# A two-layer encoder trunk on one core: the second mixer's scores as four products over all 128 rows, its rotation ended a unit later, its outputs turned in three parts, and the first mixer's mask added on VectorE

## The chip, the core and the metric

The kernel runs on one core of a Trainium2 chip. The metric is device time in microseconds (us) of one execution of the whole program. The kernel before takes 1678.19 us, the median of 3 runs (1677.85 to 1679.21). All times below are of that kernel.

The engines: TensorE (PE in the profile; PEld is its weight load) multiplies and turns blocks, VectorE (DVE) and ScalarE (ACT) work element by element on PSUM and SBUF, GpSimd (POOL) and SyncE (SP) mostly issue DMAs here. Each engine runs its own instructions in a fixed order and waits for the others by semaphores.

## What is computed

Two sequences (256 and 512 rows, held as six tiles of 128 rows: tiles 0 and 1, tiles 2 to 5) go through two layers. Each layer is a token mixer and a SwiGLU, both between norms:

```python
for i in range(DEPTH):                       # DEPTH = 2
    h = rms_norm(x, norm_mix_pre[i])
    if i % 2 == 0:
        m = window_gqa_sink(h, a_w_in, a_w_o, a_sinks)     # first mixer
    else:
        m = diff_attention(h, b_w_in, b_w_o, ...)          # second mixer
    x = x + rms_norm(m, norm_mix_post[i])
    h = rms_norm(x, norm_ffn_pre[i])
    x = x + rms_norm(swiglu(h, ffn_w_gate_up[i], ffn_w_down[i]), norm_ffn_post[i])
```

```python
# first mixer: 16 query heads, 4 key heads of 64; only |q - k| <= 128 counts
sc = where(valid, q @ k.T, -inf)
m = maximum(max(sc), sink)
p = exp(sc - m) / (sum(exp(sc - m)) + exp(sink - m))
o = p @ v
# second mixer: 8 heads, each with two query and key components c of 64 and values of 128
p_c = softmax(q_c @ k_c.T)                   # all keys of the sequence
o = (p_0 - lam * p_1) @ v
o = rms_norm(o, subln) * (1 - lambda_init)   # per head
```

Everything is float32. A large product is made of three fp32r products of a high and a low part each: hi*hi, lo*hi, hi*lo.

## The kernel before

**Order.** The program is recorded as Python functions called one after the other; a scheduler then places each engine's instructions by the recorded order and by when it thinks their operands are ready. So the lists of steps in `mixer_a` and `mixer_b` set the order, and the scheduler moves rows a little. Products of 128 x 384 or 128 x 512 are the filling ("fill"), and the steps of attention are put in between them.

**First mixer** (`mixer_a`, lines 598 to 766). 24 units, one for each group of heads `gi` and tile `t`, project queries, keys and values into a PSUM bank `pqa`. Four units later a unit's attention runs as four items, one for each head. An item is `score`: two products (L661, L662) of queries with the keys' high and low parts into a bank `sc` of 256 or 384 columns (384 for tiles 3 and 4, which have a block on both sides), and one or two mask products (L664, L666): identity times a bf16 triangle of -3e38, added into the same bank. Then VectorE takes the row maximum (L668) and turns it into `negm` (L671), ScalarE takes the exponential out of PSUM with a running sum (L677) and the sink's exponential (L679). `normalize` (L686 to L688) follows one item later, `turn_e` (L697, transposes `tpe`) two items after that, and `values` (L711, `poa`) once for each unit.

**Second mixer** (`mixer_b`, lines 796 to 990). `b_fill` lists 50 units: `rotated` units project a head's queries or keys for half of the rows (bank `pqb` or `pkb`), `straight` units project values for a group of heads (`pvb`). When a rotated unit ends, ScalarE copies it out as `xq` or `xk` (L834), four DMAs from GpSimd's queue swap its quarters (L836), and VectorE forms z = s cos + r sin (L838, L839, L840), where L839 needs the four DMAs. ScalarE then rounds z to the high part (L849). For queries VectorE puts the low part into the other 64 rows (L852). For keys two DMAs copy the high part into the other 64 rows (L855) and VectorE writes the low part (L856) to its own 64 rows alone.

`score` (L879) of a head and tile makes two banks `bsc`, one for each component: a product over all 128 rows with the keys' high part (L890), which covers q_hi and q_lo at once, and one over 64 rows with the keys' low part (L893); the second component's 64 rows are the other half of the array. Then come the maximum (L896), exponential (L898), the combination of both components (L901 to L906), `turn_e` (L918, L920) and `values` (L931). After heads 3, 6 and 7 the heads so far are scaled on GpSimd (`rstd_sub` L391, `ob` L944). The list `events` says in which unit, counted in units and fractions, each score, turn and value step stands.

The outputs `o` are then turned into `h_hi` and `h_lo` as operands of the output projection (`transposes`, L438, L445, L446; bank `tp_o`), heads 0 to 3 first (`early`) and heads 4 to 7 later (`late`). What remains of the attention stands between the first products of that projection (`out`, bank `po`) in a list written out by hand (`run`).

Of the kernel before, what the change touches and what calls it, by code (L numbers as in the profile page):

```python
# [9 lines left out]
F32 = mybir.dt.float32  # L10
F32R = mybir.dt.float32r
# [6 lines left out]
P = 128  # L18
# [49 lines left out]
def trunk(  # L68
# [40 lines left out]
    ident_b = const.tile([P, P], BF16, name="ident_b")  # L109
    nc.vector.tensor_copy(out=ident_b, in_=ident)  # L110

    masks = []
    for name, step, mult in (("mask_l", 1, -1), ("mask_r", -1, 1)):
        m = const.tile([P, P], BF16, name=name)
        nc.gpsimd.memset(m, 0.0)
        nc.gpsimd.affine_select(
            out=m, in_=m, compare_op=ALU.is_ge, fill=MASK, base=0,
            pattern=[[step, P]], channel_multiplier=mult,
        )
        masks.append(m)  # L120
    cos_sb = const.tile([P, 4, HD], F32, name="cos_sb")
    sin_sb = const.tile([P, 4, HD], F32, name="sin_sb")
# [10 lines left out]
    def small_inputs():  # L133
# [4 lines left out]
        lam_in = const.tile([P, 4, HD], F32, name="lam_in")  # L138
# [5 lines left out]
    def small_tables():  # L144
# [3 lines left out]
        lprod = const.tile([P, 2, HD], F32, name="lprod")  # L148
# [449 lines left out]
    def mixer_a(gp, g_next, first_steps, o):  # L598
        with ExitStack() as st:
# [53 lines left out]
            def score(i, j):  # L653
# [6 lines left out]
                left, right = k0 < t, k1 > t + 1  # L660
                nc.tensor.matmul(s, q[i][:, j], kh[gi, first][:, keys], start=True, stop=False)  # L661
                nc.tensor.matmul(s, q[i][:, j], kl[gi, first][:, keys], start=False, stop=not (left or right))  # L662
                if left:
                    nc.tensor.matmul(s[:, :P], ident_b, masks[0], start=False, stop=not right)  # L664
                if right:
                    nc.tensor.matmul(s[:, (nk - 1) * P:], ident_b, masks[1], start=False, stop=True)  # L666
                mx = small.tile([P, 1], F32, tag="mx", name=f"mx{i}_{j}")
                nc.vector.tensor_reduce(out=mx, in_=s, axis=AX.X, op=ALU.max)  # L668
                h = gi * 4 + j
                negm = small.tile([P, 1], F32, tag="negm", name=f"negm{i}_{j}")  # L670
                nc.vector.tensor_scalar(  # L671
                    out=negm, in0=mx, scalar1=-HD ** -0.5, scalar2=nsink[:, h:h + 1], op0=ALU.mult, op1=ALU.min)
                if j % 2 == 0:
                    e2[0] = new_y(f"e{i}_{j}")
                e = e2[0][:, j % 2 * 512:j % 2 * 512 + nk * P]
                den = small.tile([P, 2], F32, tag="den", name=f"den{i}_{j}")
                nc.scalar.activation(  # L677
# [864 lines left out]
```

## Time and profile before

| what | us |
|---|---|
| median of 3 runs | 1678.19 |
| the profiled execution, its own time | 1678.24 |
| its span, first to last instruction | 1676.5 |
| first mixer's attention, about | 34 to 254 of the span |
| second mixer: units with attention | 833 to 1078 |
| second mixer: rest of the attention with the first output products | 1078 to 1135 |
| both SwiGLU parts, about | 299 to 780 and 1182 to 1676 |

Times within the profile are us from the span's start. In a timeline row stand the start, the time that the row covers, the engine, the line, the operation, output and inputs, the shape, how many instructions were merged, and in brackets the idle time of the engine before the row and what ended it. Matmuls overlap: what one costs the stream is the distance from its start to the next start, not its duration. In a row of groups stand the busy time of the group, the mean duration of one in ns, and the idle time before its members. In a row of waits stand who waited for whom, the sum, how often, and the longest.

### The profile page before, as it was taken

The page shows a single profiled execution, that of the slowest core. Times are in us where ns is not written, and L with a number is a line of the kernel's source. Part 1 is how long each engine was busy: PE and PEld are TensorE (multiplying, and loading weights), DVE is VectorE, ACT ScalarE, POOL GpSimd, SP SyncE. Part 2 cuts the span into 40 slices and gives each one's busy share as a digit, 9 for nine tenths or more (in the row PEclk, how much of TensorE's full clock was granted, in tenths as well). Part 3 has the DMA queues.
Part 4 walks back from the last instruction along what each step waited for, and adds up shares of the span by engine and source line. Part 5 has one row for each costly group of instructions (what it writes and reads, how often), then busy time and mean ns, then how long its engine had stood idle before and what let it go on. Part 6 is the DMA issues. An engine that isn't in the chain of part 4 may idle for free. (4 is left out here: it accounts for less than half of the span.)

```text
span 1676.5 us, 25190 instructions
## 1 busy us (share of the span) xinstructions
PE 1638.5 (98%) x9291; PEld 1495.1 (89%) x9291; DVE 1235.2 (74%) x2210; ACT 943.9 (56%) x2080; POOL 162.5 (10%) x276
## 2 busy tenths in 40 slices
PE   7999999999999999999999999999899999999998
PEld 7888878899999998888999989877899999998886
DVE  7888776896766656988685775765897666666985
ACT  6777775654444444556566666675744444444653
POOL 1000001000000000001330451331000000000000
PEclk9999999999999999999999999999999999999999
DMA  5111014534233337675432322314434343337664
GB/s 214 39 39 47 15 39 148 179 131 143 101 127 108 129 125 246 225 268 192 127 84 61 76 71 75 104 31 139 166 119 147 104 142 109 129 115 242 237 244 156
DMA packets 68187, 217.53 MB, mean 130 GB/s; under 512 B 9248, under 2 KB 13472, under 8 KB 67808
## 3 DMA queue, kind: packets, MB, share of 16 engines
q1 hardware_dynamic: 54576, 175.93, 30.9%
q0 software_dynamic: 13344, 39.73, 8.1%
q8 instruction: 73, 1.20, 0.3%
q14 instruction: 50, 0.41, 0.1%
q10 hardware_dynamic: 144, 0.26, 0.0%
HBM read 163.59 MB, written 42.86 MB: 123 GB/s over the span
## 5 line engine op out<-in xcount | busy, mean ns | idle before, releaser
L254 DVE TENSOR_TENSOR wlo<-wraw,whi 128x1024 fp32r<-128x1024 f32 (+2 forms) x174 | 204.6, 1179 | 176.7 <-ACT whi L253 175.2
L253 ACT CAST whi<-wraw 128x1024 fp32r<-128x1024 f32 (+2 forms) x174 | 175.8, 1012 | 119.9 <-PE py L347 59.1
L346 PE MATMUL py<-hhi,whi 128*128 128x384 f32 x464 | 155.4, 335 | 0.9 <-ACT u L1029 0.9
L348 PE MATMUL py<-hhi,wlo 128*128 128x384 f32 x464 | 155.0, 334 | 0.0
L347 PE MATMUL py<-hlo,whi 128*128 128x384 f32 x464 | 155.0, 334 | 0.0
L334 ACT CAST hhi<-araw 128x768 fp32r<-128x768 f32 (+1 forms) x74 | 57.6, 783 | 88.7 <-DMA araw<-act 85.9
L348 PE MATMUL pv<-whi,hlo 128*128 128x512 f32 (+1 forms) x240 | 92.2, 384 | 0.4 <-DVE hlo L335 0.4
L346 PE MATMUL pv<-whi,hhi 128*128 128x512 f32 (+1 forms) x240 | 92.4, 385 | 0.0
L347 PE MATMUL pv<-wlo,hhi 128*128 128x512 f32 (+1 forms) x240 | 92.2, 384 | 0.0
L335 DVE TENSOR_TENSOR hlo<-araw,hhi 128x768 fp32r<-128x768 f32 (+1 forms) x74 | 65.3, 890 | 32.3 <-ACT hhi L334 32.2
L346 PEld LDWEIGHTS py<-hhi,whi 128*128 128x128 f32 x464 | 87.1, 188 | 1.8 <-ACT u L1029 1.5
L347 PEld LDWEIGHTS py<-hlo,whi 128*128 128x128 f32 x464 | 87.1, 188 | 0.0
L348 PEld LDWEIGHTS py<-hhi,wlo 128*128 128x128 f32 x464 | 87.1, 188 | 0.0
L346 PE MATMUL po<-whi,hhi 128*128 128x512 f32 x192 | 78.8, 410 | 3.3 <-ACT hhi L445 2.9
L1082 POOL DMA_DIRECT2D act<-st x22 | 19.4, 882 | 635.9 <-DVE st L1081 635.9
L347 PE MATMUL po<-wlo,hhi 128*128 128x512 f32 x192 | 75.4, 393 | 0.8 <-DVE wlo L254 0.8
L348 PE MATMUL po<-whi,hlo 128*128 128x512 f32 x192 | 76.0, 396 | 0.2 <-DVE hlo L335 0.2
L346 PE MATMUL pqa<-whi,hhi 128*128 128x384 f32 x192 | 73.7, 384 | 0.0
L346 PE MATMUL px<-hhi,whi 128*128 128x384 f32 x208 | 70.2, 339 | 2.7 <-ACT hhi L334 2.7
L898 ACT ACTIVATE be<-bsc,bmx 128x512 f32<-128x512 f32 (+1 forms) x96 | 58.5, 614 | 24.6 <-DVE bmx L896 24.3
L347 PE MATMUL px<-hlo,whi 128*128 128x384 f32 x208 | 70.0, 337 | 1.2 <-DVE hlo L335 1.2
L391 POOL TENSOR_TENSOR rstd_post<-rstd_post,mhalf 128x1 f32<-128x1 f32 x23 | 16.4, 716 | 557.9 <-ACT rstd_post L390 557.9
(315 smaller groups left out, 5112.9 us busy)
## 6 DMA issues: line engine op xcount, KB each, us to landing
act<-st POOLq DMA_DIRECT2D x22, 1344.0 KB, 6.6
wraw<-in_wgu SPq DMA_DIRECT2D x56, 512.0 KB, 4.6
araw<-act SPq DMA_DIRECT2D x70, 384.0 KB, 4.1
y_wraw<-in_wgu SPq DMA_DIRECT2D x40, 512.0 KB, 3.8
wraw<-in_wd SPq DMA_DIRECT2D x40, 512.0 KB, 4.0
xd<-x SPq DMA_DIRECT2D x18, 512.0 KB, 3.0
x<-xd SPq DMA_DIRECT2D x18, 512.0 KB, 3.9
wraw<-in_wo SPq DMA_DIRECT2D x16, 512.0 KB, 3.5
```

What stands on the lines that cost most here:

```text
L253: state["raw_hi"] = nc.scalar.copy(out=hi, in_=src)
L254: state["raw_lo"] = nc.vector.tensor_tensor(out=lo, in0=src, in1=hi.bitcast(F32), op=ALU.subtract)
L334: state["hi"] = nc.scalar.copy(out=hi, in_=src)
L335: state["lo"] = nc.vector.tensor_tensor(out=lo, in0=src, in1=hi.bitcast(F32), op=ALU.subtract)
L346: nc.tensor.matmul(out, ah, bh, start=start and i == 0, stop=False, skip_group_check=more)
L347: nc.tensor.matmul(out, ah, bl, start=False, stop=False, skip_group_check=more)
L348: nc.tensor.matmul(out, al, bh, start=False, stop=stop and i == last, skip_group_check=more)
L391: nc.gpsimd.tensor_tensor(out=r[:, :w], in0=r[:, :w], in1=mhalf[:, :w], op=ALU.pow)
L898: nc.scalar.activation(out=e[:, :n * P], in_=s, func=AF.Exp, bias=mx, accum_out=den[:, c:c + 1])
L1082: nc.gpsimd.dma_start(out=at_hand[c // 4][:, :, c // 2 % 2], in_=out.pop(c // 2))
```

## The change

1. **Mask.** The mask products go. A float32 tile `mask` of 128 x 384 holds the two triangles with zeros between, and one VectorE instruction with a running minimum, `tensor_tensor_reduce`, reads the scores and the mask, writes (sc + mask) * -1/8 to SBUF and gives `negm`. ScalarE's exponential reads that tile instead of PSUM. The sink's exponential, its sum and the reciprocal are made once for two heads, in `normalize`, which now stands at every second item for the pair before; `turn_e` stays three items behind its score. Small tables move into a pool that is freed behind the first mixer.
2. **Scores of the second mixer.** The key tile has four parts, high and low for each component. The low part is copied to the other 64 rows too (DMAs of 64 x 2 x 384 in place of 64 x 384, issued behind the subtraction), and each bank gets two products over all 128 rows. Value tiles: 8 buffers in place of 9.
3. **Rotation.** `end` of a rotated unit stops behind the first product with the cosine. The rest runs at the end of the next unit, set behind the last combination on VectorE.
4. **Turns.** `o` is turned in three parts: heads 0 to 3, 4 to 6, and 7. The first parts of tiles 0 to 2 stand in the units 48 and 49; score events stand 0.2 to 0.8 units later, and `run` is a new list.

```diff
-                left, right = k0 < t, k1 > t + 1
-                nc.tensor.matmul(s, q[i][:, j], kl[gi, first][:, keys], start=False, stop=not (left or right))
-                if left:
-                    nc.tensor.matmul(s[:, :P], ident_b, masks[0], start=False, stop=not right)
-                if right:
-                    nc.tensor.matmul(s[:, (nk - 1) * P:], ident_b, masks[1], start=False, stop=True)
-                nc.vector.tensor_reduce(out=mx, in_=s, axis=AX.X, op=ALU.max)
-                nc.vector.tensor_scalar(
-                    out=negm, in0=mx, scalar1=-HD ** -0.5, scalar2=nsink[:, h:h + 1], op0=ALU.mult, op1=ALU.min)
-                nc.scalar.activation(
-                    out=e, in_=s, func=AF.Exp, bias=negm, scale=HD ** -0.5, accum_out=den[:, 0:1])
-                nc.scalar.activation(out=den[:, 1:2], in_=negm, func=AF.Exp, bias=sink[:, h:h + 1])
+                nc.tensor.matmul(s, q[i][:, j], kl[gi, first][:, keys], start=False, stop=True)
+                nc.vector.tensor_tensor_reduce(
+                    out=e, in0=s, in1=mask[:, side:side + nk * P], scale=-HD ** -0.5, scalar=nsink[:, h:h + 1],
+                    op0=ALU.add, op1=ALU.min, accum_out=negm[:, c])
+                nc.scalar.activation(out=e, in_=e, func=AF.Exp, bias=negm[:, c], scale=-1.0, accum_out=den[:, c])
...
             def normalize(i, j):
+                nc.vector.tensor_tensor(out=den[:, 2:4], in0=negm, in1=sink[:, h:h + 2], op=ALU.add)
+                nc.scalar.activation(out=den[:, 2:4], in_=den[:, 2:4], func=AF.Exp)
+                nc.vector.tensor_tensor(out=den[:, 0:2], in0=den[:, 0:2], in1=den[:, 2:4], op=ALU.add)
+                nc.vector.reciprocal(out=den[:, 0:2], in_=den[:, 0:2])
+                for c in range(2):
+                    e = blocks[i, j + c][0]
+                    nc.vector.tensor_scalar(out=e, in0=e, scalar1=den[:, c:c + 1], scalar2=None, op0=ALU.mult)
...
-                if 1 <= n <= n_items:
-                    normalize(*items[n - 1])
+                if n % 2 == 0 and 2 <= n <= n_items:
+                    normalize(*items[n - 2])
...
-                            nc.gpsimd.dma_start(out=b[other], in_=b[rows])
-                            nc.vector.tensor_tensor(
-                                out=kk[h][rows, 2, cols], in0=z[rows], in1=b[rows].bitcast(F32), op=ALU.subtract)
+                                c = 2 * (rows is down)
+                                nc.vector.tensor_tensor(
+                                    out=kk[h][rows, c + 1, cols], in0=z[rows], in1=b[rows].bitcast(F32), op=ALU.subtract)
+                                nc.gpsimd.dma_start(out=kk[h][other, c:c + 2, cols], in_=kk[h][rows, c:c + 2, cols])
...
+                    state["mark"] = state["z"]
+                    waiting.append(rest)
...
-                    vv[g, t] = ap.tile([P, n], F32, tag="v", name=f"vb{g}_{t}", bufs=9)
+                    vv[g, t] = ap.tile([P, n], F32, tag="v", name=f"vb{g}_{t}", bufs=8)
...
-                    nc.tensor.matmul(ss[c], qt[:, c, at], kk[h][:, c, keys], start=True, stop=False)
-
-                for c, rows in enumerate((slice(0, HD), slice(HD, P))):
-                    nc.tensor.matmul(ss[c], qt[rows, c, at], kk[h][rows, 2, keys], start=False, stop=True)
+                    for part in range(2):
+                        nc.tensor.matmul(
+                            ss[c], qt[:, c, at], kk[h][:, 2 * c + part, keys], start=part == 0, stop=part == 1)
...
-            turn_o = [transposes(o[t], t, f"o1_{t}", subl) for t in range(NT)]
+            turn_o = [[turn_heads(t, *hs) for hs in ((0, 4), (4, 7), (7, 8))] for t in range(NT)]
...
+            def turn_heads(t, k0, k1):
...
+                    for j in range(n):
+                        nc.tensor.transpose(tp[:, j * P:(j + 1) * P], o[t][:, (k0 + j) * P:(k0 + j + 1) * P], ident)
+                    nc.scalar.activation(out=h4, in_=v, func=AF.Copy, scale=subl)
+                    nc.vector.scalar_tensor_tensor(
+                        out=l4, in0=v, scalar=subl, in1=h4.bitcast(F32), op0=ALU.mult, op1=ALU.subtract)
...
+            events += [(48.3 + t / 2, "o", t) for t in range(3)]
...
+                late = waiting[:]
+                waiting.clear()
                 for s in placed(att, [int((at - i) * len(fill)) for at, _, _ in now], fill):
                     s()
+                turned(late)
```

What this moves on the engines, at three places:

VectorE in the first mixer, unit 10 (tile 4, 384 columns): `mx10_1` is the maximum of head 1, `sp` belongs to the projection, `den10_0` and `y_e10_0` to the sum and exponentials of head 0 (and 1). Before:

```order
L668 TENSOR_REDUCE mx10_1_1922<-sc10_1_1917 128x1
L627 TENSOR_TENSOR sp13_1884<-qk13_1877,sp13_1884 128x4x64
L629 TENSOR_TENSOR sp13_1884<-qk13_1877,sp13_1884 128x128
L671 TENSOR_SCALAR negm10_1_1924<-mx10_1_1922,nsink_108 128x1
L686 TENSOR_TENSOR den10_0_1900<-den10_0_1900 128x1
L687 RECIPROCAL den10_0_1900<-den10_0_1900 128x1
L688 TENSOR_SCALAR y_e10_0_1899<-y_e10_0_1899,den10_0_1900 128x384
L668 TENSOR_REDUCE mx10_2_1948<-sc10_2_1943 128x1
```

And now, where each `ISA` pair is the new instruction and its reading out:

```order
L667 ISA y_e10_0_1677,negm10_0_1678<-sc10_1_1699,mask_91,nsink_107 128x384
L667 ISA negm10_0_1678 128x1
L678 TENSOR_TENSOR den10_0_1679<-negm10_0_1678,sink_106 128x2
L624 TENSOR_TENSOR sp13_1668<-qk13_1661,sp13_1668 128x4x64
L626 TENSOR_TENSOR sp13_1668<-qk13_1661,sp13_1668 128x128
L667 ISA y_e10_2_1718,negm10_2_1719<-sc10_2_1715,mask_91,nsink_107 128x384
L667 ISA negm10_2_1719 128x1
L680 TENSOR_TENSOR den10_0_1679<-den10_0_1679 128x2
L681 RECIPROCAL den10_0_1679<-den10_0_1679 128x2
L684 TENSOR_SCALAR y_e10_0_1677<-y_e10_0_1677,den10_0_1679 128x384 x2
```

The scaling of head 0 stood ahead of the third head's maximum; now it stands behind the third head's masked minimum, together with head 1's.

GpSimd in the second mixer, where head 5's keys are rotated (`xk5_0`, `xk5_1`) while heads 0 to 3 of the tiles 3 and 4 are scaled (`rstd_sub21`, `ob3`, and so on). Before:

```order
L836 DMA xk5_0_10729<-xk5_0_10729 32x384 x2
L836 DMA xk5_1_10815<-xk5_1_10815 32x384
L855 DMA kb5_10739<-kb5_10739 64x384 x2
L391 TENSOR_TENSOR rstd_sub22_10802<-rstd_sub22_10802,mhalf_102 128x4
L836 DMA xk5_1_10815<-xk5_1_10815 32x384
L944 TENSOR_TENSOR ob4_8521<-ob4_8521,rstd_sub22_10802 128x512
L836 DMA xk5_1_10815<-xk5_1_10815 32x384 x2
```

And now:

```order
L834 DMA xk5_0_10172<-xk5_0_10172 32x384 x4
L388 TENSOR_TENSOR rstd_sub21_10225<-rstd_sub21_10225,mhalf_101 128x4
L963 TENSOR_TENSOR ob3_8008<-ob3_8008,rstd_sub21_10225 128x512
L834 DMA xk5_1_10256<-xk5_1_10256 32x384 x4
L388 TENSOR_TENSOR rstd_sub22_10308<-rstd_sub22_10308,mhalf_101 128x4
L963 TENSOR_TENSOR ob4_8009<-ob4_8009,rstd_sub22_10308 128x512
L858 DMA kb5_10266<-kb5_10266 64x2x384 x2
```

The four DMAs of `xk5_1` had a key copy, a power and a scaling between them; now they follow each other, and the key copies stand two tiles later.

TensorE at the end of the second mixer, around the first product of the output projection (`po1_0_0`). Before:

```order
L893 MATMUL bsc40_1_11839<-kb6_11432,qb6_1_11360 128x512
L438 MATMUL tp_o1_0_0_11855<-ident_81,ob0_8517 128x128 x4
L918 MATMUL tpa38_11862<-ident_81,be38_11696 128x128 x4
L931 MATMUL pob37_11869<-vb2_0_10892,aT37_11780 128x128
L931 MATMUL pob37_11869<-vb2_1_10949,aT37_11780 128x128
L438 MATMUL tp_o1_1_0_11879<-ident_81,ob1_8518 128x128 x4
L346 MATMUL po1_0_0_11833<-whi158_11209,hhi0_111 128x512
```

And now, the rows ahead of that product:

```order
L895 MATMUL bsc39_0_11305<-kb6_10993,qb6_1_10913 128x512 x2
L895 MATMUL bsc39_1_11306<-kb6_10993,qb6_1_10913 128x512 x2
L937 MATMUL tpa37_11322<-ident_81,be37_11185 128x128 x2
L950 MATMUL pob36_11327<-vb2_0_10372,aT36_11262 128x128
L950 MATMUL pob36_11327<-vb2_1_10437,aT36_11262 128x128
L343 MATMUL po1_0_0_11300<-whi158_10697,hhi0_110 128x512
```

The transposes `tp_o1_0_0`, whose result that product reads, stood five rows ahead of it and now stand 71 rows ahead, among the products of unit 48.

More of the change, by code (lines that the diff above doesn't have):

```diff
@@ L108, in trunk @@
     nc.vector.tensor_copy(out=ident_r, in_=ident)
[L109 to L115, printed above, removed]
+    early_stack = ctx.enter_context(ExitStack())
+    early = early_stack.enter_context(tc.tile_pool(name="early", bufs=1, side="right", reuse_waits="tile"))
+    mask = early.tile([P, 3 * P], F32, name="mask")
+    nc.gpsimd.memset(mask, 0.0)
+    for at, step, mult in ((0, 1, -1), (2 * P, -1, 1)):
         nc.gpsimd.affine_select(
-            out=m, in_=m, compare_op=ALU.is_ge, fill=MASK, base=0,
+            out=mask[:, at:at + P], in_=mask[:, at:at + P], compare_op=ALU.is_ge, fill=MASK, base=0,
             pattern=[[step, P]], channel_multiplier=mult,
         )
-        masks.append(m)
-    cos_sb = const.tile([P, 4, HD], F32, name="cos_sb")
-    sin_sb = const.tile([P, 4, HD], F32, name="sin_sb")
+    cos_sb = early.tile([P, 4, HD], F32, name="cos_sb")
+    sin_sb = early.tile([P, 4, HD], F32, name="sin_sb")
     mhalf = const.tile([P, 8], F32, name="mhalf")
@@ L673, in score @@
                 if j % 2 == 0:
[L674 to L677, printed above, removed]
-                    out=e, in_=s, func=AF.Exp, bias=negm, scale=HD ** -0.5, accum_out=den[:, 0:1])
-                nc.scalar.activation(out=den[:, 1:2], in_=negm, func=AF.Exp, bias=sink[:, h:h + 1])
-                blocks[i, j] = e, den
@@ L682, in mixer_a @@
-            e2 = {}
-            def normalize(i, j):
-                e, den = blocks[i, j]
-                nc.vector.tensor_tensor(out=den[:, 0:1], in0=den[:, 0:1], in1=den[:, 1:2], op=ALU.add)
-                nc.vector.reciprocal(out=den[:, 0:1], in_=den[:, 0:1])
-                nc.vector.tensor_scalar(out=e, in0=e, scalar1=den[:, 0:1], scalar2=None, op0=ALU.mult)
+                    pair[0] = (
+                        new_y(f"e{i}_{j}"), small.tile([P, 2], F32, tag="negm", name=f"negm{i}_{j}"),
+                        small.tile([P, 4], F32, tag="den", name=f"den{i}_{j}"))
@@ new lines, in score @@
+                blocks[i, j] = e, den, negm
+            pair = {}
+            def normalize(i, j):
+                h = (i // NT) * 4 + j
+                _, den, negm = blocks[i, j]
+                nc.vector.tensor_tensor(out=den[:, 2:4], in0=negm, in1=sink[:, h:h + 2], op=ALU.add)
[5 more added lines that the diff above has]
+                    nc.vector.tensor_scalar(out=e, in0=e, scalar1=den[:, c:c + 1], scalar2=None, op0=ALU.mult)
@@ L806, in mixer_b @@
             live = [0]
+            waiting = []
             def held(key, n):
@@ L848, in end @@
[L848 to L857 removed]
+                    state["z"] = nc.vector.tensor_tensor(out=z, in0=s, in1=tab[0][:, half], op=ALU.mult)
```

87 lines of the change are left out of this document (52 added, 35 removed).

## The prediction

> **What bounds the kernel now.** I read the page's table of engines first, then the table by windows for the three stretches that the change touches, then TensorE's waits there.
>
> ```profile
> PE 1638.5 (98%) x9291; PEld 1495.1 (89%) x9291; DVE 1235.2 (74%) x2210; ACT 943.9 (56%) x2080; POOL 162.5 (10%) x276
> ...
> 34.00:254.00 220.00, 219.46 (x1503) 183.54 (x1502) 172.42 (x634) 165.96 (x573) 0.00 (x0) 1.00 0.11 36
> 833.00:1078.00 245.00, 239.62 (x1448) 219.05 (x1446) 176.40 (x350) 156.13 (x426) 78.47 (x144) 0.99 0.28 76
> 1078.00:1135.00 57.00, 53.01 (x301) 42.87 (x300) 35.03 (x69) 40.01 (x121) 20.11 (x30) 0.97 0.17 54
> ```
>
> A window's row gives its length, then the busy time of PE, PEld, DVE, ACT and POOL, the granted clock, the DMA share and GB/s. TensorE is the bound: 98% of the span, and in the first mixer 219.5 of 220 us. So an instruction taken out of its stream shortens the program by its place in it, as long as nothing else comes late. It idles in the second mixer: 5.4 us in the second window and 4.0 us in the third. The next rows are its waits from 833 to 1135, and from 34 to 254 the one of a turn:
>
> ```profile
> PE tpa L918 <- ACT aT L920: 4.1, 1, 4.1
> PE po L346 <- ACT hhi L445: 2.9, 1, 2.9
> PE pob L931 <- ACT aT L920: 1.2, 2, 1.0
> PE tpa L918 <- DVE be L906: 0.7, 2, 0.4
> ...
> PE tpe L697 <- DVE den L686: 0.2, 1, 0.2
> ```
>
> Four entries make 8.9 us in the second mixer. The first mixer's turns wait 0.2 us in all, so its attention chain is hidden now.
>
> **The masks.** What one costs the stream is the distance to the next start. Here are a block with one mask, then one with two:
>
> ```profile
> 130.98 0.28 PE L662 MATMUL sc<-kla,qa 128*128 128x256 f32 x1
> 131.10 0.23 PE L664 MATMUL sc<-mask_l,ident_b 128*128 128x128 bf16 x1
> 131.17 0.50 PE L697 MATMUL tpe<-ident,y_e 128*128 128x128 f32 x3
> ...
> 119.89 0.23 PE L664 MATMUL sc<-mask_l,ident_b 128*128 128x128 bf16 x1
> ...
> 120.02 0.50 PE L697 MATMUL tpe<-ident,y_e 128*128 128x128 f32 x3
> ...
> 121.75 0.23 PE L664 MATMUL sc<-mask_l,ident_b 128*128 128x128 bf16 x1
> ```
>
> One mask takes 131.17 - 131.10 = 0.07 us, two 0.13. A head has eight of them (one each for tiles 0, 1, 2 and 5, two for 3 and 4), 16 heads 128: 128 x 0.065 = 8.3 us. Some end a little earlier where a projection follows; I take **-8.0 us**.
>
> **The scores of the second mixer.** A 512-column block, a 256-column block, and two full products of 512 columns elsewhere:
>
> ```profile
> 910.18 0.63 PE L890 MATMUL bsc<-kb,qb 128*128 128x512 f32 x2
> 910.73 0.49 PE L893 MATMUL bsc<-kb,qb 64*128 64x512 f32 x2
> 911.16 0.44 PE L918 MATMUL tpa<-ident,be 128*128 128x128 f32 x2
> ...
> 903.46 0.40 PE L890 MATMUL bsc<-kb,qb 128*128 128x256 f32 x2
> ...
> 904.11 0.66 PE L918 MATMUL tpa<-ident,be 128*128 128x128 f32 x4
> ...
> 1150.14 0.39 PE L346 MATMUL po<-whi,hhi 128*128 128x512 f32 x1
> 1150.37 0.40 PE L347 MATMUL po<-wlo,hhi 128*128 128x512 f32 x1
> ...
> PEld bsc L893 <- issue: 11.1, 31, 0.4
> ```
>
> The 512 block takes 911.16 - 910.18 = 0.98 us; two full products alone would be 0.46, so the pair over 64 rows costs 0.52, more than the two full ones that replace it. The last row says where: the load of the first 64-row weights stood still 31 times, 11.1 us, up to 0.4 each. After the change it is 4 x 0.23 = 0.92: -0.06, times 32 blocks -1.9 us. The 256 block takes 0.65; a full product of 256 columns takes 131.10 - 130.98 = 0.12, four 0.48: -0.17, times 16 blocks -2.7 us. Together **-4.6 us**.
>
> [...]
>
> **The waits of the second mixer.** The longest one, with VectorE, ScalarE and GpSimd ahead of it and TensorE behind:
>
> ```profile
> 999.49 1.32 DVE L839 TENSOR_TENSOR xk<-xk,rope 128x384 f32<-128x384 f32 x1 [2.44 <-DMA xk<-xk]
> ...
> 1001.43 1.04 ACT L849 CAST kb<-zk 64x384 fp32r<-64x384 f32 x2 [4.77 <-DVE zk L840]
> ...
> 997.73 0.50 POOL L836 DMA_DIRECT2D xk<-xk  x1 [1.57 <-issue]
> ...
> 1002.93 1.00 PE L918 MATMUL tpa<-ident,be 128*128 128x128 f32 x4 [4.10 <-ACT aT L920]
> ...
> 1006.03 0.52 PE L347 MATMUL pvb<-wlo,hhi 128*128 128x384 f32 x1
> 1006.35 0.41 PE L348 MATMUL pvb<-whi,hlo 128*128 128x384 f32 x1
> 1006.60 0.33 PE L346 MATMUL pvb<-whi,hhi 128*128 128x384 f32 x1
> 1006.77 0.34 PE L347 MATMUL pvb<-wlo,hhi 128*128 128x384 f32 x1
> ...
> DVE xk L839 <- DMA xk<-xk: 19.4, 9, 4.7
> ```
>
> The last quarter's DMA was issued at 997.73, behind GpSimd's scaling. VectorE stood at L839 for it, with the next score's maximum queued behind; ScalarE stood at L849 behind that, with `aT` queued; TensorE waited 4.1 us. Then it ran slower for 3.5 us: products stand 0.32 us apart up to 1006.35 and 0.17 from 1006.60 on, and the four transposes took 1.00 us where they take 0.66 (904.11). With some five products, the transposes and the values between them that is about 1.6 us more. The same VectorE wait recurs nine times, 19.4 us, and stands ahead of the 1.0 us wait too. After the change L839 runs a unit later, and a unit of 24 products alone is 24 x 0.17 = 4.1 us; the four DMAs follow each other on GpSimd. What is late next is the end of the rotation: L839, L840, two roundings, two subtractions, then the copies, about 6 us (six steps of 0.5 to 0.6, as the 1.04 for two roundings, and a copy that is issued and lands in some 2.5, the 1.8 from 997.73 to 999.49 and its own issue). Head 3 has least room: its last keys are finished behind unit 28, its scores begin at 30.3, and those that need both halves of the keys stand two blocks later, two units in all, over 8 us. So I count no new wait. The 2.9 us wait is the output projection at a turn recorded right ahead of it; now 71 rows lie between. Sum: 8.9 us of waits and about 3 of slow clock behind the two long ones (1.6 measured, the other like it), 11.9. The bounds are 0 and -12.5 gained. Turns become 18 pairs of ScalarE and VectorE work in place of 12, in a stretch where ScalarE is 70% busy (40.0 of 57), so I leave 0.9 for short waits: **-11 us**.
>
> **The first mixer's chain.** VectorE loses maximum and `negm`, and gets the fused instruction with its reading out, which no row shows. Its nearest rows:
>
> ```profile
> L668 DVE TENSOR_REDUCE mx<-sc 128x1 f32<-128x256 f32 (+1 forms) x96 | 44.5, 465 | 12.8 <-PE sc L666 8.6 <-PE sc L664 3.3
> L671 DVE TENSOR_SCALAR negm<-mx,nsink 128x1 f32<-128x1 f32 x96 | 20.1, 210 | 0.2
> L906 DVE SCALAR_TENSOR_TENSOR be<-be,rho 128x512 f32<-128x512 f32 x32 | 24.6, 768 | 1.0
> L906 DVE SCALAR_TENSOR_TENSOR be<-be,rho 128x256 f32<-128x256 f32 x16 | 7.7, 484 | 0.5
> ...
> L677 ACT ACTIVATE y_e<-sc,negm 128x384 f32<-128x384 f32 x32 | 18.8, 587 | 4.6 <-DVE negm L671 4.4
> L679 ACT ACTIVATE den<-negm,sink 128x1 f32<-128x1 f32 x96 | 28.5, 296 | 0.0
> ...
> L688 DVE TENSOR_SCALAR y_e<-y_e,den 128x384 f32<-128x384 f32 x32 | 13.4, 419 | 0.9
> ...
> 102.10:110.60 8.50, 8.29 (x60) 7.09 (x58) 7.60 (x29) 6.94 (x25) 0.00 (x0) 1.00 0.45 132
> ```
>
> A two-operand instruction takes 0.48 at 256 columns and 0.77 at 512 (L906), so about 0.62 at 384; with 0.2 for the reading out it equals what goes (0.465 + 0.21), and the pairwise sums save a little. VectorE's load stays. Its deadline does not. Two items are 121.75 - 119.89 = 1.86 us apart, 1.73 without masks. Before, head 0's exponentials were scaled alone and turned three items on, over 5 us later. Now they wait for head 1's sum: from that score's start to the turn stand two items and 0.35 of the third's products, 3.8 us, less 0.5 until the scores are there: 3.3 us. The chain: fused 0.62 + 0.2, exponential 0.59 + 0.2, sink's exponential 0.30, sum and reciprocal 0.2 each (as L671), scaling 0.42: 2.7 us, without the five hand-overs between engines. **The margin is at most 0.6 us**, where some 2.5 were left. The second pair of a unit has about 1 us more, as value products stand before its turn. In the fullest units VectorE is busy 7.6 of 8.5 us (last row), so what is queued in front of a chain shows at once. Bounds: no wait, or 0.5 us for each of 24 first pairs, 12 us. Since the scheduler puts projections ahead of a turn that it thinks late, I take a third: **+4 us**.
>
> **At nothing.** ScalarE's 48 saved small exponentials lie beside TensorE (ScalarE 166 of 220 us). The mask's setup on GpSimd takes the place of two smaller ones of the same kind. Twice the bytes in 32 small copies lie in 28% DMA share. With 8 value buffers two copies wait for an earlier head's values, holding two of eight PSUM banks; ScalarE is 64% busy there (156 of 245). Uncovered, these would cost 1 to 2 us.
>
> **Sum.** The profiled execution took 1678.24 us (span 1676.5, 1.7 around it), the median 1678.19, so no shift: 1678.2 - 8.0 - 4.6 - 11 + 4 = **1658.6 us**.
>
> **Rivals.** (a) The first mixer becomes bound by its chain: every first pair waits 0.5 us and the fuller units more, 14 us; for it the margin of 0.6, against it VectorE's 22% idle there: 1678.2 - 8 - 4.6 - 11 + 14 = 1668.6. (b) The waits of the second mixer only move, to keys that come a unit later or to short waits at the turns; for it the 6 us chain: no -11, 1669.6. [...]
>
> **How the numbers follow.** Forecast 0.65 (1652 to 1665), (a) 0.17, (b) 0.09, (c) 0.07, (d) 0.02. The low end is every wait gone and no new one, 1678.2 - 8.3 - 4.6 - 12.5 = 1652.8, and a little; the high end takes in (a), (b) and (d): 1652 to 1673. Faster by over 0.2% (below 1674.8; a measurement can tell about that much) is the forecast, (a), (b) and (d), less what tails cross the line: 0.88; same 0.06; slower 0.06.
>
> **What would show it.** Masks: no L664 and L666, and about 8 us less from the first to the last `sc`. Scores: four `bsc` products 0.23 us apart, no 64-row load standing still. Rotation: VectorE's wait for `xk` near nothing, and no wait of `tpa` or `po` over 1 us from 833 to 1135. [...] I am wrong if the first mixer does not shorten at all, or if new waits of `bsc` for `kb` appear.

## The result, and the profile after

The changed kernel takes 1656.97 us, the median of 4 runs (1655.73 to 1658.87), beside 1678.7 us for the kernel before in the same comparison: a ratio of 0.987, with a 95% interval of 0.9853 to 0.9887. The profiled execution took 1656.38 us, its span 1654.4.

The table of engines of the changed kernel (busy us, share, instructions), then its three windows: the first mixer, the second mixer's units, and the rest of its attention beside the first output products. Columns are as in the prediction.

```profile
PE 1618.3 (98%) x9163; PEld 1499.3 (91%) x9163; DVE 1222.8 (74%) x2167; ACT 934.4 (56%) x2038; POOL 170.7 (10%) x275
```

```profile
34.00:248.00 214.00, 210.42 (x1372) 179.75 (x1371) 161.40 (x586) 157.05 (x525) 0.00 (x0) 1.00 0.12 37
830.00:1058.00 228.00, 228.00 (x1430) 222.02 (x1428) 172.13 (x343) 153.30 (x416) 80.03 (x140) 1.00 0.35 91
1058.00:1115.00 57.00, 52.94 (x306) 45.46 (x305) 36.11 (x77) 41.10 (x133) 20.32 (x30) 0.97 0.21 61
```

TensorE is busy for the whole of the second window now, where it idled 5.4 us before; in the first it idles 3.6 us, before 0.5. The third still idles 4.1. The waits of TensorE name them: the first four rows are the first mixer, the next two the second; the last row is VectorE's wait for the swapped keys, 19.4 us before.

```profile
PE tpe L693 <- DVE y_e L684: 1.8, 4, 0.7
PE po L345 <- DVE hlo L332: 0.9, 2, 0.7
PE po L343 <- ACT hhi L331: 0.6, 1, 0.6
PE poa L707 <- ACT eT L697: 0.2, 1, 0.2
...
PE tpa L937 <- DVE be L909: 2.7, 1, 2.7
PE tp_o L921 <- POOL ob L963: 1.3, 1, 1.3
...
DVE xk L839 <- DMA xk<-xk: 1.2, 2, 1.0
```

The groups of the first mixer, shapes apart (busy us, then mean ns of one): the fused instruction and its reading out.

```profile
L667 DVE CUSTOM_DVE_ANT_0 y_e<-sc,mask,nsink 128x256 f32<-128x256 f32 x64 | 30.6, 479 | 9.8 <-PE sc L658 9.1
...
L667 DVE CUSTOM_DVE_ANT_0 y_e<-sc,mask,nsink 128x384 f32<-128x384 f32 x32 | 19.7, 614 | 8.3 <-PE sc L658 7.8
...
L667 DVE DVE_READ_ACCUMULATOR2_ANT negm<- 128x1 f32 x96 | 7.9, 83 | 0.0
```

0.48 and 0.61 us, as estimated; the reading out takes 0.08, not 0.2. The timeline of a 256-column block and of a 512-column block in the second mixer:

```profile
897.05 0.64 PE L895 MATMUL bsc<-kb,qb 128*128 128x256 f32 x4
897.52 0.60 PE L937 MATMUL tpa<-ident,be 128*128 128x128 f32 x4
...
910.32 1.10 PE L895 MATMUL bsc<-kb,qb 128*128 128x512 f32 x4
911.25 0.38 PE L937 MATMUL tpa<-ident,be 128*128 128x128 f32 x2
911.47 0.61 PE L950 MATMUL pob<-vb,aT 128*128 128x128 f32 x4
```

A block takes 0.47 (897.52 - 897.05) and 0.93 us, before 0.65 and 0.98. The two transposes behind it take 0.22 (911.47 - 911.25), before 0.27 (911.43 - 911.16; the first start is in the prediction, the second here). That second difference was in no term of the prediction.

```profile
911.43 1.06 PE L931 MATMUL pob<-vb,aT 128*128 128x128 f32 x8
```

Where the time went, by stages (starts of rows in the traces, us; the second mixer's two parts belong together):

| profiled execution of | first `sc` to last `poa` | first `pkb` to last `pob` | to layer 2's first `pz` |
|---|---|---|---|
| before | 218.5 | 330.1 | 78.5 |
| changed | 212.9 | 315.6 | 76.7 |
| e5, mask and scores | 212.9 | 326.4 | 77.8 |
| e3, changed, rotation at once | 212.9 | 326.0 | 76.7 |
| e4, changed, turns at use | 213.0 | 319.0 | 78.9 |
| e12, changed, pair again | 213.1 | 322.4 | 77.0 |
| e6, changed, a maximum more | 224.1 | 314.2 | 76.9 |
| e7, changed, turn later | 214.5 | 314.5 | 76.9 |
| e8, changed, tail | 213.1 | 313.6 | 75.2 |

The first mixer gave 5.6 us, the second 14.6 + 1.8 = 16.4. Each row is one execution. Stages outside these differ by up to some 4 us between profiled executions of the same steps (the stretch from the last `poa` to the first `pkb` takes 540.2 us in e10 and 544.3 in e7), so kernels are compared by stage.

The second mixer's two stages can be taken apart further. "Idle" is the time in which TensorE stood still. "Half clock" is half of its busy time in the stretches that were granted half the clock, an estimate of what these cost. The rest is its products at the full clock:

| profiled execution of | both stages | idle | half clock | rest |
|---|---|---|---|---|
| before | 408.7 | 13.0 | 3.4 | 392.3 |
| changed | 392.3 | 6.9 | 1.6 | 383.8 |
| e2, scores | 404.1 | 13.4 | 4.1 | 386.6 |
| e5, mask and scores | 404.1 | 11.7 | 7.5 | 384.9 |
| e3, changed, rotation at once | 402.7 | 11.7 | 5.7 | 385.4 |
| e4, changed, turns at use | 397.9 | 10.4 | 1.7 | 385.8 |
| e12, changed, pair again | 399.4 | 6.9 | 1.7 | 390.9 |
| e8, changed, tail | 388.8 | 4.6 | 0.0 | 384.2 |

So 8.5 of the second mixer's 16.4 us are products that got shorter, and 7.9 are waits and the half clock behind them.

### The profile page after: what moved, and what is told of

The parts are those of the page before. It is cut to its first block, busy times and chain, and to the rows that moved or that the text cites. A ratio compares the mean times of both kernels' runs of the same rounds, so it can differ in the third digit from the quotient of the medians.

```text
span 1654.4 us, 24784 instructions
## 1 busy us (share of the span) xinstructions
PE 1618.3 (98%) x9163; PEld 1499.3 (91%) x9163; DVE 1222.8 (74%) x2167; ACT 934.4 (56%) x2038; POOL 170.7 (10%) x275
## 5 line engine op out<-in xcount | busy, mean ns | idle before, releaser
L1114 POOL DMA_DIRECT2D act<-st x22 | 19.4, 882 | 636.6 <-DVE st L1113 636.6
L388 POOL TENSOR_TENSOR rstd_post<-rstd_post,mhalf 128x1 f32<-128x1 f32 x23 | 20.3, 885 | 544.9 <-ACT rstd_post L387 544.9
L344 PE MATMUL po<-wlo,hhi 128*128 128x512 f32 x192 | 75.2, 392 | 0.0
```

The source lines that it names most:

```text
L344: nc.tensor.matmul(out, ah, bl, start=False, stop=False, skip_group_check=more)
L388: nc.gpsimd.tensor_tensor(out=r[:, :w], in0=r[:, :w], in1=mhalf[:, :w], op=ALU.pow)
L1114: nc.gpsimd.dma_start(out=at_hand[c // 4][:, :, c // 2 % 2], in_=out.pop(c // 2))
```

## The experiments

Medians in us. Ratios are against the kernel before, run beside each group.

| kernel | median | before | ratio, 95% interval |
|---|---|---|---|
| changed | 1656.97 | 1678.7 | 0.987 (0.9853 to 0.9887) |
| e1 mask only | 1670.62 | 1678.21 | 0.9952 (0.9938 to 0.9965) |
| e2 scores only | 1673.55 | 1678.21 | 0.997 (0.9959 to 0.9981) |
| e3 rotation at once | 1667.25 | 1678.21 | 0.9929 (0.9917 to 0.9942) |
| e4 turns at use | 1663.42 | 1678.21 | 0.9907 (0.9893 to 0.9921) |
| e5 mask and scores | 1667.59 | 1679.49 | 0.9923 (0.9909 to 0.9937) |
| e6 maximum more | 1669.1 | 1679.49 | 0.994 (0.9921 to 0.9958) |
| e7 turn later | 1660.1 | 1679.49 | 0.9879 (0.9863 to 0.9896) |
| e8 tail | 1653.75 | 1679.49 | 0.9841 (0.9828 to 0.9855) |
| e10 queries later | 1656.11 | 1678.83 | 0.9861 (0.9847 to 0.9876) |
| e11 old times | 1657.89 | 1678.83 | 0.9874 (0.9859 to 0.989) |
| e12 pair again | 1664.17 | 1678.83 | 0.9908 (0.9891 to 0.9924) |
| e6b small more | 1658.35 | 1678.83 | 0.9878 (0.9863 to 0.9894) |

### One part alone: mask (e1), scores (e2)

e1 puts part 1 of the change, word for word, into the kernel before; e2 puts part 2 there, with the copies of the keys' low part, 8 value buffers and the pool of small tables. Its products:

```diff
-                    nc.tensor.matmul(ss[c], qt[:, c, at], kk[h][:, c, keys], start=True, stop=False)
-
-                for c, rows in enumerate((slice(0, HD), slice(HD, P))):
-                    nc.tensor.matmul(ss[c], qt[rows, c, at], kk[h][rows, 2, keys], start=False, stop=True)
+                    for part in range(2):
+                        nc.tensor.matmul(
+                            ss[c], qt[:, c, at], kk[h][:, 2 * c + part, keys], start=part == 0, stop=part == 1)
```

> The kernel before with the first part of the change alone (mask added on VectorE, sums for two heads). My theory: the 128 mask products take 8.0 us with them and the shorter margin of the turns gives 1.8 us back (the tpe waits in the changed kernel), so 1.6 to 2.2 us of tpe waits, last score at about 239.5 us of the span, and the whole 6 us shorter than before: about 1672.5. Rival: the first mixer's gain in the changed kernel is partly owed to something else or is lost again at the first output projection: 1674 to 1677. Rival (a) of the prediction, the chain as the new bound: no gain, 1678 or more.

> The kernel before with the second part alone: keys' low part copied to the other 64 rows, four products over 128 rows for a score, 8 value buffers, the small tables in a pool that is freed. My theory: 32 blocks of 512 columns by 0.06 us and 16 of 256 by 0.17 us, 4.6 us shorter than before: about 1673.7. The copies of the keys now wait for the subtraction and the rotation still stands where it was, so up to 2 us may be lost on keys that come late. [...] Rival, what the products give moves into the waits of the second mixer, since a score is no wait's cause: 1677 to 1679.

e1 fits the theory: 1670.6, a little better than 1672.5, with the first mixer at 212.8 us and the same four waits for `tpe`, 1.8 us, as the changed kernel. The first mixer's result is that of the mask alone. It is 5.6 of e1's 7.6 us. Most of the rest came in the second mixer, whose steps e1 doesn't touch: its two stages take 405.9 us, 2.8 less than before, and the wait of `tpa` is 2.4 us there in place of 4.1. Why it got shorter is open.

e2 is 4.7 us shorter than before, the number expected, but that is luck: the products gave more (5.7 us by the table above), and waits took a part back. Among TensorE's waits of e2 from 815 to 1125 are these:

```profile
PE pob L934 <- ACT be L901: 2.0, 1, 2.0
PE bsc L895 <- ACT xk L837: 1.8, 1, 1.8
PE bsc L895 <- DMA kb<-kb: 1.3, 2, 0.9
```

These three are new. In the last row scores come before their keys, which are now copied behind the subtraction; the other two wait for ScalarE, and that the rotation holds up its queue is argued, not shown. e12 shows that the products are worth more than 4.7 when keys are not late.

### The delay and the turns, undone one at a time and together (e3, e4, e5)

```diff
-                    state["mark"] = state["z"]
-                    waiting.append(rest)
+                    rest()
```

The diff is e3's. e4 records each turn ahead of the products that use it (two of the places):

```diff
-            run = S(6, 3) + T(6, 1) + V(6, 0) + out[0][:2] + [lambda: turned(late)] + S(6, 4) + T(6, 2) + V(6, 1) + out[0][2:4]
+            run = S(6, 3) + T(6, 1) + V(6, 0) + O(0, 0) + out[0][:2] + [lambda: turned(late)] + S(6, 4) + T(6, 2) + V(6, 1) + out[0][2:4]
...
-            run += S(7, 2) + T(7, 0) + V(6, 5) + out[0][4:7] + O(2, 1)
+            run += S(7, 2) + T(7, 0) + V(6, 5) + O(0, 1) + out[0][4:7]
```

e5 is e1 and e2 in one kernel: rotation, times of the scores and turns as before.

> The changed kernel with the rotation of a unit ended at once, as before, all else as changed (events, four products, turns in three parts). My theory: VectorE waits for xk again (19 us before, 1.2 in the changed kernel), TensorE waits for tpa or pob again for 4 to 6 us with about 2 us of slow clock behind them: 6 to 8 us longer than the changed kernel, 1663 to 1665. Rival: the later events and the shorter products took these waits away, not the delay: within 2 us of the changed kernel, 1656 to 1659, VectorE's waits for xk there or not.

> The changed kernel with the turns of the outputs recorded right ahead of the products that use them, all else as changed. My theory: each of the nine turns of tiles 0 to 2 is waited for, the longest near the 2.9 us of before, several others 0.5 to 1.5 us, less what the scheduler moves by itself: 4 to 9 us longer than the changed kernel, 1661 to 1666, with new waits of po for hhi or hlo. Rival: the one long wait of before was queue order at that place alone, and three parts at their use cost nothing more: 1656 to 1659.

> The kernel before with the first two parts together; rotation, events and turns as before. It closes a square: both later parts undone (this), turns alone (e3, 1667.3), delay alone (e4, 1663.4), both (1657.0). By the sum of e1 and e2 (7.6 and 4.7 us) it takes 1666. Theory 1, the two later parts mend different waits, and each is worth what its removal cost (10.3 and 6.5 us): 1657 + 16.8 = 1673.8. Theory 2, turns in three parts are worth nothing while the rotation still holds up the queues, and the delay alone gives 2 to 3 us: 1665 to 1667, with the long wait of tpa near 1000 us of the span and the wait of po for a turn both there.

TensorE's waits of e3, the longest of them, and VectorE's wait for `xk`; then those of e4 and of e5:

```profile
PE tpa L936 <- ACT xk L832: 2.8, 1, 2.8
PE tpa L936 <- DVE be L908: 1.9, 1, 1.9
PE po L343 <- ACT be L900: 1.4, 1, 1.4
...
DVE xk L839 <- DMA xk<-xk: 13.3, 8, 4.7
```

```profile
PE po L343 <- ACT hhi L924: 6.8, 3, 3.4
```

```profile
PE po L343 <- ACT hhi L442: 2.9, 1, 2.9
PE pob L928 <- ACT be L895: 2.0, 1, 2.0
PE bsc L889 <- ACT xk L831: 1.8, 1, 1.8
```

With the rotation ended at once, most of VectorE's wait is back, and TensorE has three long waits; e3 is 10.3 us longer than the changed kernel, more than the 6 to 8 expected. With turns at their use, three of nine are waited for, 6.8 us, and e4 is 6.5 us longer, as expected. So both parts take away the waits that they were blamed for.

But they do not add up. The second mixer with its following stage takes 404.1 us with neither (e5), 402.7 with turns and no delay (e3), 397.9 with the delay and no moved turns (e4), 392.3 with both; e3 and e4 keep the later times of the scores too, and e4 the turns' three parts. Turns alone are worth 1.4 us, the delay alone 6.2, together 11.9 (by the medians 0.3, 4.2 and 10.6). Much of this is half clock: by the table above it makes up 5.8 of the 6.2 and 5.9 of the 11.9 us, while TensorE's idle time falls by 1.3 and 4.8. That is nearer to theory 2 of e5 than to theory 1, but the delay alone gives more than its 2 to 3 us, and e5 has two waits of 2.0 and 1.8 where it foresaw the long one of `tpa`. In e3 the `po` wait goes from 2.9 to 1.4 us and changes its releaser, from a turn's `hhi` to `be` of a score. The reason that suggests itself is that turns moved forward stand in the same two queues as a rotation that still waits for its DMAs; that was not tried by itself.

### The pair over 64 rows, put back (e12)

```diff
                 for c in range(2):
-                    for part in range(2):
-                        nc.tensor.matmul(
-                            ss[c], qt[:, c, at], kk[h][:, 2 * c + part, keys], start=part == 0, stop=part == 1)
+                    nc.tensor.matmul(ss[c], qt[:, c, at], kk[h][:, 2 * c, keys], start=True, stop=False)
+                for c, rows in enumerate((slice(0, HD), slice(HD, P))):
+                    nc.tensor.matmul(ss[c], qt[rows, c, at], kk[h][rows, 2 * c + 1, keys], start=False, stop=True)
```

> The changed kernel with the keys' low parts multiplied as a pair over 64 rows again, all else as changed (the copies are made, half of them unused). My theory after reading the starts: a 512-column block takes 0.05 us more, a 256-column one 0.17, and the first transpose behind a pair stands 0.165 us ahead of the second in place of 0.109: 32 x 0.05 + 16 x 0.17 + 48 x 0.056 = 7.0 us longer, 1664. Rival 1, the block alone counts, as the prediction had it: 4.6 us, 1661.5. Rival 2, the scores of the changed kernel are covered by VectorE, which is 75% busy there, and their length does not matter: 1657 to 1658.

```profile
916.23 0.63 PE L894 MATMUL bsc<-kb,qb 128*128 128x512 f32 x2
916.78 0.49 PE L896 MATMUL bsc<-kb,qb 64*128 64x512 f32 x2
917.21 0.44 PE L937 MATMUL tpa<-ident,be 128*128 128x128 f32 x2
917.48 0.61 PE L950 MATMUL pob<-vb,aT 128*128 128x128 f32 x4
```

In this timeline of e12 the block takes 0.98 and its two transposes 0.27, as before the change. The second mixer's two stages are 399.4 us, 7.1 longer than in the changed kernel, and the medians differ by about as much. TensorE idles 6.9 us in both, and the half clock costs 1.7 and 1.6, so all of it is in the products. So the four full products are worth 7 us, 2.7 of them (48 x 0.056) at the transposes behind the pair.

### The first mixer's margin (e6, e6b, e7)

```diff
+                junk = small.tile([P, 1], F32, tag="mx", name=f"mx{i}_{j}")
+                nc.vector.tensor_reduce(out=junk, in_=s, axis=AX.X, op=ALU.max)
                 nc.scalar.activation(out=e, in_=e, func=AF.Exp, bias=negm[:, c], scale=-1.0, accum_out=den[:, c])
```

e6b has a `tensor_scalar` of 128 x 1 in place of the reduction. e7 records the turn of the item four back ahead of a score, in place of the one three back behind it:

```diff
+                cut = (n_units - 1 - LAG) * 4
+                if 4 <= n <= cut:
+                    turn_e(*items[n - 4])
                 if n < n_items:
                     score(*items[n])
...
-                if 3 <= n <= n_items + 2:
+                if cut <= n <= n_items + 2:
                     turn_e(*items[n - 3])
```

> The changed kernel with one more instruction on VectorE for each head of the first mixer, behind the fused one: the old maximum of the scores, written to a place that nobody reads (0.36 to 0.55 us, 96 times, 44.6 us in all). It prices the chain. My theory (margin used up, VectorE 161 of 214 us busy and now 206): each first pair of the 24 units waits 0.7 to 1.2 us more and the fullest units become bound by VectorE: 17 to 35 us longer, 1674 to 1692, tpe waits of 15 us or more. Rival: the turns have more room than the row of 3.3 us against 2.7 said, since the scheduler moves products ahead of a late turn: under 8 us longer, below 1665.

> The changed kernel with one small VectorE instruction more for each head of the first mixer, 128 values, 0.21 us by the row of negm in the kernel before, in the chain ahead of the exponential: half the price of e6, whose 0.46 us a head made the first mixer 11.6 us longer (waits of tpe 1.8 to 11.4 us). Theory 1, the margin is used up and each delay is paid at the first pairs: 24 x 0.2 x 2 heads would be 9.6, by e6's slope 11.6 x 0.21 / 0.465 = 5.2 us: 1661 to 1663. Theory 2, the margin is there and only the full units of e6 were bound by VectorE: 0 to 2 us, 1657 to 1659.

> The changed kernel with each turn of the first mixer recorded one item later, ahead of that item's score (the last units as before). My theory: the 1.8 us of tpe waits come from the two-item margin, so three of the four waits go and the first mixer is 1.2 to 1.8 us shorter: 1655 to 1656, unless values of a unit, which now stand right behind its last turn, wait for the copy of it: up to 24 times 0.3 us longer. Rival: the four waits come from the order at three places alone (the first unit, and the units at 105 and 156 us) and a later turn does not touch them: 1657.

TensorE's waits for turns in the first mixer, of e6, then e6b, then e7:

```profile
PE tpe L695 <- DVE y_e L686: 10.1, 11, 1.9
PE tpe L695 <- ACT whi L250: 1.3, 1, 1.3
```

```profile
PE tpe L696 <- DVE y_e L687: 3.2, 6, 0.8
```

```profile
PE tpe L693 <- DVE y_e L684: 0.4, 1, 0.4
```

In e6 and e6b the added instruction stands in VectorE's queue, but the head's own exponential doesn't wait for it; they price VectorE's load, and the chain only where it is queued behind. The price, by the first mixer's length against 212.9 us, is not a line. 0.21 us a head more (e6b; the row of L671 before) makes six waits of the four and the first mixer 0.6 us longer (213.5 us); 0.46 a head (e6; the row of L668 before) makes eleven and 11.2 us. So there is room at most places, and it ends between the two; e6 fell between its two expectations, e6b came out by theory 2. e7 took three of the four waits away, as expected, yet its first mixer is 1.6 us longer. By the distances between starts, `sc` and `poa` rows took 7.3 us more there, the others 5.7 less. The value products stand between projections 22 times in place of 13, and the first product of a score behind a turn stands 0.20 us ahead of the next, in place of 0.12. That these two make up the loss is argued, not shown. The waits that could be seen were not worth having out in this way.

### What is left at the tail (e8, e10)

The longest wait that the change leaves, in the timeline of VectorE, then of TensorE, then by windows:

```profile
1064.46 1.14 DVE L852 TENSOR_TENSOR qb<-zq,qb 64x384 fp32r<-64x384 f32 x2
1065.63 0.22 DVE L906 SCALAR_TENSOR_TENSOR rho<-rden,bden,nlam 128x1 f32<-128x1 f32 x1
1065.77 0.68 DVE L899 TENSOR_REDUCE bmx<-bsc 128x1 f32<-128x512 f32 x1
1066.37 0.74 DVE L909 SCALAR_TENSOR_TENSOR be<-be,rho 128x512 f32<-128x512 f32 x1
```

```profile
1067.26 1.09 PE L937 MATMUL tpa<-ident,be 128*128 128x128 f32 x4 [2.73 <-DVE be L909]
1068.14 1.91 PE L950 MATMUL pob<-vb,aT 128*128 128x128 f32 x8
1069.71 0.77 PE L343 MATMUL po<-whi,hhi 128*128 128x512 f32 x1
```

```profile
1067.30:1070.50 3.20, 3.20 (x14) 3.10 (x15) 3.15 (x7) 2.26 (x6) 2.06 (x2) 0.51 0.49 170
1070.50:1075.00 4.50, 4.50 (x30) 4.05 (x30) 3.49 (x10) 3.53 (x14) 2.97 (x4) 1.00 0.85 222
```

The queries' subtractions (1.14 us) and the next score's maximum stand ahead of the combination that TensorE waits for. Behind the wait the clock granted is 0.51 for 3.2 us. e8 ends the last two rotations later, and turns a tile in the output projection behind four steps of products; the two were not run apart. Its main lines:

```diff
-                turned(late)
-            late = waiting[:]
+                if i < 49:
+                    turned(late)
+            late += waiting
...
-            run = S(6, 3) + T(6, 1) + V(6, 0) + out[0][:2] + [lambda: turned(late)] + S(6, 4) + T(6, 2) + V(6, 1) + out[0][2:4]
-            run += S(6, 5) + T(6, 3) + V(6, 2) + out[1][:2] + S(7, 0) + T(6, 4) + V(6, 3) + O(0, 1) + out[1][2:4]
+            run = S(6, 3) + T(6, 1) + V(6, 0) + out[0][:2] + S(6, 4) + T(6, 2) + V(6, 1) + [lambda: turned(late[1:])] + out[0][2:4]
+            run += S(6, 5) + T(6, 3) + V(6, 2) + [lambda: turned(late[:1])] + out[1][:2] + S(7, 0) + T(6, 4) + V(6, 3) + O(0, 1) + out[1][2:4]
...
+            steps = out_unit(t, wk, o, 0, gp, sq, f"po{layer}_0_{t}")
...
+                steps[4:4] = turn_o(t + 1)
```

Here `late` holds the queries' rotation, then the keys'. e10 differs in that `turned(late[1:])`, the keys, stays ahead of `S(6, 4)`.

> The changed kernel with the last two rotations ended later (keys of head 7 behind the score of head 6, tile 4, queries behind that of tile 5) and, in the output projection, the last turn of the next tile behind four steps of products in place of ahead of them. My theory: the 2.7 us wait of tpa at 1067 us stands behind these rotations on VectorE and ScalarE, the 1.3 us wait at 1104 behind the scaling of head 7; both go, with 1.5 to 2 us of slow clock behind the first: 4 to 6 us shorter than the changed kernel, 1651 to 1653. Rival: the work only moves to the next score, and a wait like it stands some microseconds later: 1655 to 1658.

> As e8, but the last keys' rotation stands where the change has it (ahead of the score of head 6, tile 4), and only the queries' rotation waits until that of tile 5 is through. In e8 (1653.8) a score waited 1.1 us for keys of head 7 that came late, and tpa 0.8 us. My theory: the queries' two rotations steps, two roundings and subtractions (2.2 us on VectorE, 1.0 on ScalarE) are what stood ahead of the 2.7 us wait, and the keys are early enough in their old place: no bsc wait for kb, tpa at 1067 under 0.8 us, 0.5 to 1.5 us shorter than e8, 1652 to 1653.5. Rival: the keys too are part of that wait, which comes back at 1.5 us or more: as e8 or longer, 1653.5 to 1656.

TensorE's waits of e8, and then of e10, from 815 on:

```profile
PE bsc L895 <- DMA kb<-kb: 1.1, 1, 1.1
PE tpa L937 <- DVE rden L904: 0.8, 1, 0.8
```

```profile
PE tpa L937 <- DVE be L909: 1.5, 1, 1.5
PE pob L950 <- DVE hlo L925: 1.0, 1, 1.0
PE tpa L937 <- ACT ob L954: 0.7, 1, 0.7
```

e8 is the fastest kernel here: 1653.75 us, ratio 0.9841. Its two stages take 388.8 us, 3.5 less than in the changed kernel, 1.6 of it by the half clock that is gone; the median lies between the theory's range and the rival's, and the intervals of the two ratios still touch. e10's theory fell: the keys' rotation is part of that wait, which comes back at 1.5 us with two others, and the time is nearly that of the change.

### The later times of the scores (e11)

```diff
-                    (0, 12.7, 17), (1, 17, 22.5), (2, 22.5, 29.3), (3, 30.3, 35.1), (4, 35.1, 40.5), (5, 40.5, 46.3)):
+                    (0, 12, 16.7), (1, 16.7, 22.2), (2, 22.2, 28.8), (3, 29.6, 34.8), (4, 34.8, 40.3), (5, 40.3, 46)):
-            events += [(48.7 + t / 2, "s", 6 * NT + t) for t in range(3)]
+            events += [(47.9 + t / 2, "s", 6 * NT + t) for t in range(3)]
```

> The changed kernel with the score steps at the times that they had before (12 to 46 and from 47.9, in units), the rotation still a unit later. It tests the room that the prediction counted on (a rotation's 6 us chain behind a unit's end against over 8 us until the keys are needed). My theory: with 0.2 to 0.8 of a unit (0.8 to 3.3 us) less, heads 0, 2 and 3 start on keys or queries that are not there: waits of bsc for kb or qb, 1 to 3 us each at two or three places, 3 to 8 us longer than the changed kernel, 1660 to 1665. Rival: the room is enough without the later times, which only set the order: within 1.5 us, 1655.5 to 1658.5.

```profile
PE bsc L895 <- DMA kb<-kb: 2.2, 3, 0.9
```

Scores do wait for keys, at three places, 2.2 us in all (0.9 at most), but the tail's waits shrink meanwhile, and the median is within the rival's range. The later times keep such waits away; they are not where the gain is.

## Why the prediction was right, point by point

The forecast of 1658.6 us stands 1.6 from the 1656.97 measured, and the mechanisms named did act. That it comes so close is in part luck: the two terms of the second mixer were off by 3 to 4 us each, in opposite directions.

**Masks, -8.0.** Right. The distances behind the 128 mask products in the kernel before sum to 7.8 us; the first mixer is 5.6 shorter, and e1 alone has all of it.

**First mixer's chain, +4.** Right in kind, too large. 7.8 - 5.6 leaves 2.2. TensorE's idle time there rose by 3.0: 1.8 for `tpe`, as the margin of two items said, and the rest nearly all for `hhi` and `hlo` of the first output products, which the prediction did not name. Some 0.8 us of other gain is not assigned. The 4 was a third of a bound and no sum. "At most 0.6" of margin was too tight a reading: four pairs of 24 wait.

**Scores of the second mixer, -4.6.** The mechanism was right, the term mis-sized. The block itself gave 32 x 0.05 + 16 x 0.17 = 4.3. The first transpose behind a pair gave 48 x 0.056 = 2.7 more, as the starts in the traces of before and e12 have it (0.165 us to the second transpose, 0.109 without a pair). e12 measured 7.1; the products of the two stages got 8.5 shorter in all, so 1.4 is not assigned. The step that failed was to end the sum at the next instruction's start, when that instruction carried part of the price.

**Waits, -11.** The mechanism was right at both places: the wait behind the swapped keys and the one for a turn are gone. The term was too large. From before to changed TensorE idles 6.1 us less in the two stages, and the half clock costs 1.8 less: 7.9. What failed is "no wait of `tpa` or `po` over 1 us": a wait of 2.7 us with half the clock behind it is left, behind the last rotations, while the prediction looked for late keys at head 3, and one of 1.3 (`tp_o`) at the scaling on GpSimd. From e5 to the changed kernel the same edits give 11.9 us, with other times of the scores (e11: about 1.6) among it, but e5 has 19.2 us of waits and half clock where the kernel before has 16.4, so a part of that gain only takes back what part 2 costs without the delay. The prediction also summed waits one by one, as if each edit took its own, and e3 and e5 show that the turns alone give 1.4. Its bound of 12.5 has no working; the terms shown end at 11.9. In the second mixer's sum, before to changed, 16.4 us stand against 15.6 forecast: 8.5 and 7.9 in place of 4.6 and 11.

**Rivals.** (a) did not happen: the turns wait 1.8 us. (b) did not as a whole, but waits did move: TensorE's sum to 9.2 us before and 4.0 now, all at new places. For the chances of (c) and (d) no run shows a cause: the fused instruction takes 0.48 and 0.61 us, where the rows of L906 gave 0.48 and about 0.62, and e12, with the pair over 64 rows in place of two full products, takes 7.2 us longer than the changed kernel. e6 adds 0.46 us a head to VectorE's load for 11.2 us, and still takes 0.994 of the time before. What a slower instruction ahead of the exponential itself would cost was not tried.

## What to carry to other kernels

Edits against waits that share queues did not add up here (1.4 and 6.2 us alone, 11.9 together): undo each edit alone and both together before pricing either. Price products over 64 rows over the instruction behind them too (0.056 us at each of 48 transposes here). When a wait goes, look for what the same queue holds back at the end of the stage: moving two rotations and a turn there (e8) gave another 3 to 5 us.

## What was not expected of the hardware

Some waits of TensorE cost more than their length here, as the granted clock behind them shows. Windows behind a wait, of the kernel before (4.10 us ahead), of e4 (2.53 ahead) and of e6 (1.87 ahead); the granted clock stands third from the right:

```profile
1002.90:1006.40 3.50, 3.47 (x14) 3.28 (x15) 2.17 (x6) 2.96 (x9) 0.47 (x1) 0.53 0.31 56
```

```profile
1074.73:1077.93 3.20, 2.90 (x16) 2.35 (x17) 2.41 (x6) 1.17 (x6) 2.43 (x3) 1.00 0.05 12
```

```profile
156.85:160.05 3.20, 3.20 (x23) 2.50 (x24) 2.74 (x9) 1.83 (x4) 0.00 (x0) 1.00 0.55 196
```

Behind the 4.10 us, and the 2.73 us of the changed kernel above (0.51), the clock is halved for about 3.3 us of the window, so by an estimate, half of that, some 1.6 us are added; behind 2.53 and 1.87 it is not (1.00 in both rows). The length of the wait alone does not tell these apart. In e6 a wait of 2.84 us ends at 1079.27, longer than the 2.73, and no half clock follows; the two windows that it lies in:

```profile
1074.76:1078.17 3.41, 1.66 (x8) 1.01 (x6) 3.32 (x8) 3.36 (x9) 1.46 (x2) 1.00 0.87 334
1078.17:1081.58 3.41, 2.31 (x17) 2.17 (x18) 3.37 (x8) 2.93 (x10) 1.85 (x2) 1.00 0.59 211
```

The records of the granted clock in the traces of before and changed say more. But for the one behind the last product, every stretch at half clock there lasts 3.41 us, and within a trace their starts lie whole multiples of it apart (before: 1003.10 - 299.95 = 206 x 3.4133 and 1085.02 - 1003.10 = 24 x 3.4133; changed: 1186.46 - 1067.00 = 35 x 3.4133). In the 3.41 us right ahead of these stretches TensorE idled 1.66, 3.25 and 1.52 us in before, 2.46 and 2.24 in changed. In the other steps of the same length between 40 and 1640 us, counted from those starts, it idled at most 1.53 us in either trace. The wait of 2.73 us lay in one step, the one that idled 2.46; the wait of 2.84 fell into the two rows above, which idled 1.75 (3.41 - 1.66) and 1.10. So the idle time in one step tells these cases apart better than the length of a wait does, and not fully: 1.52 us stand ahead of a half clock, 1.53 and e6's 1.75 do not.

The exponential did not gain from reading SBUF: 516 and 622 ns at 256 and 384 columns in the changed kernel, 484 and 587 from PSUM before. And the pair over 64 rows starts together (the two products are 3 to 4 ns apart in the trace of before), and still costs more than two full products: by the starts at 512 columns 0.10 us ahead of it (0.33 in place of 0.23), 0.19 behind it (0.42 in place of 0.23), and 0.056 at the transposes.
